# A two-layer recurrent trunk on one core: the o and v projections of head groups 2 and 3 as seven block products in place of eight, with the residual kept in DRAM

## The chip, the cores and the metric

The kernel runs on one core of one Trainium2 chip. The metric is the device time of one execution in microseconds. The kernel before takes 1529.73 us, the median of 3 runs (1529.43 to 1530.63).

## What is computed

Input `x` has 256 tokens of 2048 channels. Two layers follow, each a matrix-memory branch (A) and a gated linear recurrence (B) side by side, and then a last RMS norm. Everything is float32. Cut to what matters:

```python
def hybrid_layer(x, ...):
    u = rms_norm(x, norm_g)
    p = u @ w_in                              # 2048 x 12304
    qk, v, o, z_a, ig, fg, xb, z_b = split(p) # 2048 each; ig, fg 8 each
    q, k = split(silu(causal_dwconv(qk, qk_conv)))
    h = mlstm_chunkwise(q, k, v, ig + i_bias, log_sigmoid(fg + f_bias))
    h = h * sigmoid(o)
    y_a = norm_per_head(h) * head_norm_g * silu(z_a)
    xc = causal_dwconv(xb, lru_conv_w) + lru_conv_b
    y_b = rg_lru(xc, w_a, b_a, w_x, b_x, lam) * silu(z_b)
    return x + concat(y_a, y_b) @ w_out       # 4096 x 2048

def reference(x, ...):
    for l in range(2): x = hybrid_layer(x, ...)
    return rms_norm(x, final_g)
```

The o and v of the diff are the columns of `w_in` that give the output gate `o` and the values `v`. There are 8 heads of 256 columns, worked on as 4 groups g of 2 heads, so o and v of one group are two products of the same 256 x 2048 left factor with 2048 x 512.

## The kernel before, in words

**Weights.** All weights lie in DRAM as units of 1 MB (`ws[u]`, 128 partitions x 2048), in the order in which the kernel uses them. The queue of SyncE (SP) loads one unit after another into `raw`, three buffers of 1 MB (L204). A unit is two halves of 128x1024. `prepare` (L209) splits each half into two numbers of lower precision: ScalarE (ACT) casts it to `wH` (L222) and VectorE (DVE) subtracts that from `raw`, which leaves `wL` (L223, recorded as L111, the line of the helper `tt_`). `wH` and `wL` have four buffers each, so a half's buffer is the one of the half four places earlier, and a cast or a subtraction waits until TensorE (PE) is through with that one. The main loop prepares three halves ahead.

**Products.** A product of float32 numbers is three products of split numbers: high x high, high x low and low x high. `mm_a` (L238 to L240; o, v, z and the output projection) keeps a 128x128 block of the activations in the array and streams 512 columns of weights: 12 matmuls of 512 columns for a half. `mm_b` (L255 and L257; qk, xb and zb) keeps the weights and streams the activations: 8 pairs of a 512 and a 256 column matmul for a half. o, v, z, qk, xb and zb are chunks of 4 units each; one chunk of the output projection is 2 units.

**Accumulators.** The 8 PSUM banks are two pairs `acc` (128 x 2 x 512) for the chunks and four single banks for everything else. A chunk takes the pair that the chunk before it does not have.

**Order.** `_plan` (L31) lists the chunks. For each layer and group: o, v, qk, one chunk of the output projection of the group before, xb, a second, z, gate, a third, zb, a fourth. What follows a chunk is its post (`o_post` L432, `v_post` L442, `qk_post` L457, `z_post` L525, `gate_half` L583, `zb_post` L648); the longer ones are generators, which the main loop advances a little after each half (`pump`). The residual stays in SBUF: `out_chunk` (L685) adds its accumulator into `x_acc` (128 x 2 x 2048) on DVE. `y_a` and `y_b`, the left factors of the output projection, have two buffers each (`yaH`, `yaL`, `ybH`, `ybL`). `gate_half` makes the two gates of the recurrence: for each of 8 blocks of 128x256 matmuls of 512 and 256 columns, a bias on ACT (L601), an addition on DVE, and one sigmoid over 1024 columns (L604).

From this a scheduler makes the order of instructions of each engine. An engine takes its own in that order, one after another.

Of the kernel before, what the change touches and what calls it, by code (L numbers as in the profile page):

```python
# [27 lines left out]
AHEAD = 3  # L28


def _plan():  # L31
    plan = []
    for l in range(DEPTH):
        for g in range(NG):
            fill = [("out", l, g - 1, c) for c in range(4)] if g > 0 else []
            late = [("in", l, "zb", 0)]
            plan += [("in", l, "o", g)] + (late if g == 1 else []) + [("in", l, "v", g), ("in", l, "qk", g)]
            plan += fill[0:1] + [("in", l, "xb", g)] + fill[1:2] + [("in", l, "z", g), ("gate", l, g)]
            if g > 0:
                plan += fill[2:3] + [("in", l, "zb", g)] + fill[3:4]  # L40
        if l + 1 < DEPTH:
            plan += [("out", l, NG - 1, c) for c in range(4)]
        else:
            plan.append(("last", l, NG - 1))
    return plan
# [3 lines left out]
def tile_trunk(ctx, tc, x, xt, par, gw, gb, ws, final_g, out):  # L49
# [10 lines left out]
    ps_main = ctx.enter_context(tc.tile_pool(name="ps_main", bufs=2, space=PSUM))  # L60
    ps_aux = ctx.enter_context(tc.tile_pool(name="ps_aux", bufs=4, space=PSUM))

    def aux(name):
        return ps_aux.tile([P, 512], F32, tag="aux", name=name)
# [5 lines left out]
    x_acc = act.tile([P, 2, D], F32, tag="xacc", name="x_acc")  # L70
# [15 lines left out]
    def load_x(c):  # L86
# [6 lines left out]
        nc.sync.dma_start(out=x_acc[:, :, cs], in_=xv[:, :, cs])  # L93
        square_sum(c)
        if c == 3:
            st["x_in"] = True
# [9 lines left out]

    gwp = const.tile([P, KT, 104], F32R, name="gwp")
    G.memset(gwp.bitcast(F32), 0.0)
# [12 lines left out]
    def log1p_exp_half(x_, tl):  # L121
        """returns q with log1p(exp(-|x|)) = 2 q"""
# [64 lines left out]
    st = {"nload": 0, "credit": 0.0}  # L187

    def load_unit(n):
        raw = wraw.tile([P, 2048], F32, tag="raw", name="raw")  # L190
        u = st["nload"]
        st["nload"] += 1
        if n < 4:
# [9 lines left out]
    def add_unit(mms, before=None, after=None):  # L203
        box = {}  # L204
        for i in range(2):
            halves.append(dict(box=box, i=i, mm=mms[i], split=None,
                               before=before if i == 0 else None, after=after if i == 1 else None))

    def prepare(hf):  # L209
        n = len(xT_parts) if hf["i"] == 0 else 1  # L210
        if hf["i"] == 0:
            hf["box"]["raw"] = load_unit(n)
            if n < 4:
                split_xT(0, n, xT_parts[n], range(4 * n, 4 * n + 4))
            if 4 <= st["nload"] < 8:
                load_x(st["nload"] - 4)
# [4 lines left out]
        for o in range(0, 1024, w):  # L221
# [39 lines left out]
    def chunk_in(l, kind, g, postfn, beforefn=None):  # L261
        def make_acc():
            box = {}

            def acc():
                if "t" not in box:
                    box["t"] = ps_main.tile([P, 2, 512], F32, tag="acc", name="acc")
# [43 lines left out]
    def square_sum(c):  # L311
        for t in range(2):
            junk = work.tile([P, 512], F32, tag="sF", name="junk")
            S.activation(out=junk, in_=x_acc[:, t, 512 * c : 512 * c + 512], func=AF.Square,
# [27 lines left out]
    def gates(l):  # L342
        gr = gwr[l]
        for s in range(2):
            hs, ls = slice(32 * s, 32 * s + 8), slice(64 + 32 * s, 72 + 32 * s)
            S.copy(out=gwp[:, :, hs], in_=gr[:, :, 8 * s : 8 * s + 8])
            tt_(gwp[:, :, ls], gr[:, :, 8 * s : 8 * s + 8], gwp.bitcast(F32)[:, :, hs], ALU.subtract)

    def gates_mm(l):
        ps = aux("ps_g")  # L350
        o = ps[0:104, 0:T]
        for kt in range(KT):
            PE.matmul(o, gwp[:, kt, :], st["x"][:, kt, 0, :], start=kt == 0, stop=False)
            PE.matmul(o, gwp[:, kt, :], st["x"][:, kt, 1, :], start=False, stop=kt == KT - 1)
        st["ps_g"] = ps

    def gates_gen(l):
        ps, rb = st["ps_g"], st["rb", l]

        def sc(nm):  # L360
            return small.tile([NH, T], F32, tag=f"sc_{nm}", name=f"sc_{nm}", bufs=1)
# [17 lines left out]
        sT = small.tile([64, T], F32, tag="sT", name="sT", bufs=1)  # L379
# [586 lines left out]
```

## Time and profile before

| | us |
|---|---|
| median of 3 runs | 1529.73 |
| span of the profiled execution | 1528.4 |
| PE busy | 1510.9 |
| DVE busy | 1127.6 |
| ACT busy | 885.4 |
| POOL busy | 37.6 |

The profiled execution's own time isn't given apart; its span is 1.3 us under the median of the runs, and what lies around the span is put at that. Busy shares are averages over the whole span. In a list of groups each row has the line, the engine, the operation, the tiles out<-in and the count, then busy time and the mean ns of one, then the idle time of the engine ahead of these instructions with what ended it. A row of the list of waits has the idle total, the number of waits and the longest. A row of the table of windows has the stretch, its length, the busy time of each engine with the number of instructions, the granted clock of TensorE, the share of DMA time in use and GB/s.

### The profile page before, as it was taken

Reading aid. Unit: us, or ns where it says so; the run is one execution under the profiler, and the core shown is the slowest. Engines: PE = TensorE matmul, PEld = TensorE weight load, DVE = VectorE, ACT = ScalarE, POOL = GpSimd, SP = SyncE. Lnnn points to the kernel's source line nnn. Section 1 sums busy time; section 2 is a strip of 40 time slices with the busy share of each in tenths; the row PEclk is TensorE's granted clock in tenths of the full one; section 3 lists DMA queues with packets and bytes.
Section 4 is the critical chain, followed back from the end, with each engine's and each line's share of the span. In section 5 each row is a group of like instructions: output and inputs, shape, how many; then the busy total and the mean of one; then the engine's idle time right before and its main releaser. Section 6 shows DMA issues by size and latency. Waiting matters only on the chain.

```text
span 1528.4 us, 19659 instructions
## 1 busy us (share of the span) xinstructions
PE 1510.9 (99%) x7576; PEld 1278.2 (84%) x7576; DVE 1127.6 (74%) x1594; ACT 885.4 (58%) x1141; POOL 37.6 (2%) x109
## 2 busy tenths in 40 slices
PE   8999999999999999999999999999999999999997
PEld 6888888888888888888888888888888888888885
DVE  6888867794677847778658787777847887478874
ACT  7567654674547645575555485557544575444854
POOL 0000100000000000000000001000000000000002
PEclk9999999999999999999999999999999999999998
DMA  9554655455554555445555555545555455555562
GB/s 344 192 188 164 212 185 182 173 196 194 188 190 171 191 193 193 175 183 193 175 184 180 190 176 193 193 173 192 193 193 185 173 184 197 187 182 187 171 223 102
DMA packets 45117, 288.03 MB, mean 188 GB/s; under 512 B 5072, under 2 KB 7648, under 8 KB 11744
## 3 DMA queue, kind: packets, MB, share of 16 engines
q1 hardware_dynamic: 43600, 283.40, 52.4%
q0 software_dynamic: 992, 3.16, 0.7%
q8 instruction: 59, 0.97, 0.3%
q14 instruction: 34, 0.28, 0.1%
q10 hardware_dynamic: 432, 0.23, 0.0%
HBM read 284.66 MB, written 2.11 MB: 188 GB/s over the span
## 4 chain that ended last, share of the span: by engine, by line
PE 98%; ACT 1%; DMA 0%; DVE 0%; SPq 0%; issue 0%; ACTq 0%
PE acc L255 24%; PE acc L238 18%; PE acc L240 18%; PE acc L239 18%; PE acc L257 12%; PE ps_gt L595 2%; PE ps_gt L597 1%; PE acc L788 0%; PE acc L790 0%; PE acc L789 0%; PE ps_ty L551 0%; DMA raw<-in_ws_dram 0%; PE acc_x L790 0%; PE acc_x L788 0%; PE acc_x L789 0%; PE ps_n L428 0%
## 5 line engine op out<-in xcount | busy, mean ns | idle before, releaser
L222 ACT CAST wH<-raw 128x1024 fp32r<-128x1024 f32 (+1 forms) x529 | 554.0, 1049 | 567.6 <-PE acc L240 282.6
L111 DVE TENSOR_TENSOR wL<-raw,wH 128x1024 fp32r<-128x1024 f32 (+1 forms) x529 | 643.8, 1220 | 312.3 <-ACT wH L222 311.5
L255 PE MATMUL acc<-x_s,wH 128*128 128x512 f32 x1536 | 544.1, 399 | 0.0
L257 PE MATMUL acc<-x_s,wL 128*128 128x256 f32 x1536 | 431.2, 281 | 0.0
L255 PEld LDWEIGHTS acc<-x_s,wH 128*128 128x128 f32 x1536 | 288.6, 188 | 71.0
L238 PE MATMUL acc<-wH,x_s 128*128 128x512 f32 x768 | 301.0, 392 | 6.7 <-ACT wH L222 6.7
L239 PE MATMUL acc<-wL,x_s 128*128 128x512 f32 x768 | 300.2, 391 | 0.3 <-DVE wL L111 0.3
L240 PE MATMUL acc<-wH,x_s 128*128 128x512 f32 x768 | 299.8, 390 | 0.0
L257 PEld LDWEIGHTS acc<-x_s,wL 128*128 128x128 f32 x1536 | 290.1, 189 | 0.9
L238 PEld LDWEIGHTS acc<-wH,x_s 128*128 128x128 f32 x768 | 144.7, 188 | 36.2 <-ACT wH L222 6.7
L239 PEld LDWEIGHTS acc<-wL,x_s 128*128 128x128 f32 x768 | 144.7, 188 | 30.3 <-DVE wL L111 1.2
L240 PEld LDWEIGHTS acc<-wH,x_s 128*128 128x128 f32 x768 | 144.6, 188 | 30.1
L238 PE MATMUL acc<-wH,ybH 128*128 128x512 f32 x224 | 88.1, 393 | 0.0
L238 PE MATMUL acc<-wH,yaH 128*128 128x512 f32 x224 | 87.8, 392 | 0.0
L239 PE MATMUL acc<-wL,yaH 128*128 128x512 f32 x224 | 87.4, 390 | 0.0
L240 PE MATMUL acc<-wH,yaL 128*128 128x512 f32 x224 | 87.4, 390 | 0.0
L240 PE MATMUL acc<-wH,ybL 128*128 128x512 f32 x224 | 87.3, 390 | 0.0
L239 PE MATMUL acc<-wL,ybH 128*128 128x512 f32 x224 | 87.2, 389 | 0.0
L238 PEld LDWEIGHTS acc<-wH,yaH 128*128 128x128 f32 x224 | 42.0, 188 | 9.1
L240 PEld LDWEIGHTS acc<-wH,yaL 128*128 128x128 f32 x224 | 42.1, 188 | 8.9
L240 PEld LDWEIGHTS acc<-wH,ybL 128*128 128x128 f32 x224 | 42.0, 188 | 8.8
L238 PEld LDWEIGHTS acc<-wH,ybH 128*128 128x128 f32 x224 | 42.1, 188 | 8.4
(201 smaller groups left out, 1437.2 us busy)
## 6 DMA issues: line engine op xcount, KB each, us to landing
raw<-in_ws_dram SPq DMA_DIRECT2D x260, 1024.0 KB, 4.8
raw<-in_ws_dram SPq DMA_DIRECT2D x6, 512.0 KB, 7.9
xp<-in_xt_dram SPq DMA_DIRECT2D x8, 256.0 KB, 7.4
x_acc<-in_x_dram SPq DMA_DIRECT2D x4, 512.0 KB, 9.7
nb<-nG_d POOLq DMA_DIRECT2D x8, 256.0 KB, 3.7
out_dram<-x_acc SPq DMA_DIRECT2D x8, 256.0 KB, 3.0
raw<-in_ws_dram SPq DMA_DIRECT2D x4, 256.0 KB, 6.3
fg<-in_final_g_dram POOLq DMA_DIRECT2D x2, 512.0 KB, 4.5
```

Of the source, the lines that this page charges most:

```text
L111: return V.tensor_tensor(out=o, in0=a, in1=b, op=op)
L222: S.copy(out=H[:, o : o + w], in_=r[:, o : o + w])
L238: PE.matmul(ps[:, t, :], a_H[:, kt, tsl], Hv[:, k, :], start=s, stop=False)
L239: PE.matmul(ps[:, t, :], a_H[:, kt, tsl], Lv[:, k, :], start=False, stop=False)
L240: PE.matmul(ps[:, t, :], a_L[:, kt, tsl], Hv[:, k, :], start=False, stop=e)
L255: PE.matmul(ps[:, ct, :], Hv[:, k, csl], xs[:, kt].rearrange("p a t -> p (a t)"), start=s, stop=False, skip_group_check=True)
L257: PE.matmul(ps[:, ct, T : 2 * T], Lv[:, k, csl], xs[:, kt, 0, :], start=False, stop=e, skip_group_check=True)
L595: PE.matmul(ps, Hv[:, ib, jl], xs[:, ib].rearrange("p a t -> p (a t)"), start=i == 0, stop=False, skip_group_check=True)
L597: PE.matmul(ps[:, T : 2 * T], Lv[:, ib, jl], xs[:, ib, 0, :], start=False, stop=i == 1, skip_group_check=True)
```

## The change

**Order.** `_plan` is replaced by `_sequence`, which orders units instead of chunks. A group has a head (o, zb of group 0 in group 1, and v; without o and v in groups 2 and 3) and a body: qk, two chunks of the output projection of the group before, xb, the other two, z, gate, zb. In the bodies of groups 1 and 2 stand, spread between, 16 side units: `swB` and then `swA` of the next group. After every two units of the body come one or two of them.

**Seven products for eight.** `swB` and `swA` compute o and v of group 2 or 3 together. For a pair of rows of blocks of 128 (`kp`, 8 of them) the left factor is a 2x2 array of blocks (two blocks of tokens, two of channels) and the right one too (two blocks of channels; the columns of o and those of v). Three of the seven products are in `swB` and four in `swA`, each in three terms (`sw_mm`), so a unit has 9 and 12 matmuls of 512 columns, and the eight pairs of one layer and group 168 instead of 192. The left factors' sums are made once per layer by `sw_forms` (16 operations of 1024 columns and 32 of 256 in both layers on DVE, and 8 casts on ACT), into the tile of `x_acc`. The right factors' sums are partly made in DRAM ahead of time: `stage_copy` issues 64 copies of 256 KB from DRAM to DRAM on ACT's queue and `stage_add` 64 accumulating transfers of 256 KB on POOL's; the `swA` units make two more with two additions of 128x512 on DVE. `sw_post` adds up the results: for each group 1 copy on ACT and 9 operations of 128x512 on DVE.

**PSUM.** During a pass (`swB` or `swA`) one pair `acc` and two of the four other banks belong to it, and all chunks of the body take the remaining pair. When the pass is over, the next chunk takes the pair that the pass had (`new_acc`).

**Residual in DRAM.** `out_chunk` of groups 0 to 2 copies its accumulator to `stage` (one buffer) on ACT and adds it to `xd[c]` in DRAM with an accumulating transfer of 512 KB on POOL's queue, 24 in all. Ahead of the gate of group 3 `x_acc` is loaded again on SP's queue.

**Smaller parts.** `yaH`, `yaL`, `ybH` and `ybL` have one buffer each; the tile of the gate weights is put into two of these. `gate_half` uses three matmuls of 256 columns instead of one of 512 and one of 256, and takes the sigmoid straight from PSUM, so the bias step, the addition and the wide sigmoid go. `pump`'s budget is halved in halves of a side unit.

```diff
-    ps_main = ctx.enter_context(tc.tile_pool(name="ps_main", bufs=2, space=PSUM))
-    ps_aux = ctx.enter_context(tc.tile_pool(name="ps_aux", bufs=4, space=PSUM))
+    psum = ctx.enter_context(tc.tile_pool(name="psum", bufs=1, space=PSUM))
+    def aux(name):
+        st["aux"] = 1 if st["sw"] else 1 - st["aux"]
+        return psum.tile([P, 512], F32, tag=f"aux{st['aux']}", name=name, bufs=2)
+    def new_acc():
+        st["pair"] = 1 - st["sw"]["pair"] if st["sw"] else 1 - st["pair"]
+        return psum.tile([P, 2, 512], F32, tag=f"acc{st['pair']}", name="acc")
+    def sw_banks():
+        pair = 1 - st["pair"]
+        a = psum.tile([P, 2, 512], F32, tag=f"acc{pair}", name="sacc")
+        b = [psum.tile([P, 512], F32, tag="aux0", name=f"sacc{i}", bufs=2) for i in range(2)]
+        st["sw"] = {"pair": pair, "banks": [a[:, 0, :], a[:, 1, :]] + b}
...
+    def load_x_acc():
+        new_x_acc()
+        for c in range(4):
+            nc.sync.dma_start(out=st["xa"][:, :, 512 * c : 512 * c + 512], in_=xd[c])
...
+    def load_unit(n, item, j):
...
+        if item[0] == "swA":
+            uo = blocks[("in", item[1], "o", item[2]), j // 2]
+            nc.sync.dma_start(out=raw[:, 0:1024], in_=ws[uo][:, 1024 * (j % 2) : 1024 * (j % 2) + 1024])
+            nc.sync.dma_start(out=raw[:, 1024:1536], in_=pq[item[1:]][j][:, 512:1024])
+            tt_(raw[:, 0:512], raw[:, 0:512], raw[:, 1024:1536], ALU.add)
+            tt_(raw[:, 1536:2048], raw[:, 0:512], raw[:, 512:1024], ALU.add)
+            return raw
...
     def gate_half(l, g, which):
...
-                        PE.matmul(ps, Hv[:, ib, jl], xs[:, ib].rearrange("p a t -> p (a t)"), start=i == 0,
-                                  stop=False, skip_group_check=True)
-                        PE.matmul(ps[:, T : 2 * T], Lv[:, ib, jl], xs[:, ib, 0, :], start=False, stop=i == 1,
-                                  skip_group_check=True)
+                        for W, a in ((Hv, 0), (Hv, 1), (Lv, 0)):
+                            PE.matmul(o, W[:, ib, jl], xs[:, ib, a, :], start=j == 0 and i == 0 and W is Hv and a == 0,
+                                      stop=i == 1 and W is Lv, skip_group_check=True)
...
     def out_chunk(l, g, c):
...
+            if g < NG - 1:
+                stage = act.tile([P, 2, 512], F32, tag="stage", name="stage")
+                S.copy(out=stage, in_=ps)
+                G.dma_start(out=xd[c], in_=stage, accum_op=ALU.add)
+                return
...
+    def sw_mm(bank, aH, aL, H, L, first, last):
+        PE.matmul(bank, aH, H, start=first, stop=False)
+        PE.matmul(bank, aH, L, start=False, stop=False)
+        PE.matmul(bank, aL, H, start=False, stop=last)
...
+    def sw_post(l, g, which):
+        m = st["sw"]["banks"]
+        st["sw"] = None
+        if which == "B":
+            e = st["swe"] = act.tile([P, 3, 512], F32, tag="swe", name="swe")
+            S.copy(out=e[:, 0, :], in_=m[0])
+            tt_(e[:, 1, :], m[1], e[:, 0, :], ALU.subtract)
+            tt_(e[:, 2, :], m[2], e[:, 1, :], ALU.add)
+            st["credit"] -= 1.3
+            return
+        require(("lru", l, g - 1))
+        require(("ybT", l, g - 1))
+        e = st["swe"]
+        t = work.tile([P, 512], F32, tag="sC", name="swt")
+        tt_(t, e[:, 0, :], m[1], ALU.add)
+        tt_(e[:, 0, :], e[:, 0, :], m[0], ALU.add)
+        tt_(e[:, 1, :], e[:, 1, :], m[1], ALU.subtract)
+        tt_(e[:, 2, :], e[:, 2, :], m[1], ALU.subtract)
+        tt_(t, t, m[2], ALU.add)
+        tt_(e[:, 1, :], e[:, 1, :], m[2], ALU.subtract)
+        tt_(t, t, m[3], ALU.add)
...
+    def stage_copy(d, b):
+        for h in range(2):
+            S.dma_start(out=d[:, 512 * h : 512 * h + 512], in_=b[0][1])
+    def stage_add(d, b):
+        for h in range(2):
+            G.dma_start(out=d[:, 512 * h : 512 * h + 512], in_=b[h][h], accum_op=ALU.add)
...
+        if hf["i"] == 0:
+            k = (n // 2 - STAGE_FROM) // STAGE_EVERY
+            if n // 2 >= STAGE_FROM and (n // 2 - STAGE_FROM) % STAGE_EVERY == 0:
+                if k < len(staged):
+                    stage_copy(*staged[k])
+                if 0 < k <= len(staged):
+                    stage_add(*staged[k - 1])
```

**How the order of instructions moves: the end of a pass.** DVE in the changed kernel where the `swA` pass of group 2, layer 0, ends and qk of group 2 begins. `zb`, `zsg` and `ybL` are the post of zb of group 1 in two parts, `sacc_2916` is the pass's pair, `swt` and `swe` the sums of `sw_post`; `wL_3634` and `wL_3648` are the second half of the first unit of qk and the first of the second.

```order
L178 TENSOR_TENSOR wL_3634<-raw_3606,wH_3633 128x1024
L178 TENSOR_TENSOR zb_3499<-zb_3499,acc_3536 128x512
L178 TENSOR_TENSOR ybL_3501<-zb_3499,ybH_3500 128x512
L178 TENSOR_TENSOR zb_3499<-zb_3499,rb_466 128x512
L178 TENSOR_TENSOR wL_3648<-raw_3645,wH_3647 128x1024
L178 TENSOR_TENSOR zsg_3663<-zb_3499,zsg_3663 128x512
L178 TENSOR_TENSOR swt_3669<-swe_2908,sacc_2916 128x512
L178 TENSOR_TENSOR zb_3499<-zsg_3663,xc_2712 128x512
L178 TENSOR_TENSOR swe_2908<-swe_2908,sacc_2916 128x512 x2
L178 TENSOR_TENSOR ybL_3501<-zb_3499,ybH_3500 128x512
L178 TENSOR_TENSOR swe_2908<-swe_2908,sacc_2916 128x512
```

The same engine before, where v of group 2 ends and its qk begins (`wL_3315` is the first half of qk):

```order
L111 TENSOR_TENSOR wL_3297<-raw_3278,wH_3296 128x1024
L111 TENSOR_TENSOR wL_3315<-raw_3312,wH_3314 128x1024
L111 TENSOR_TENSOR wL_3331<-raw_3312,wH_3330 128x1024
L111 TENSOR_TENSOR wL_3349<-raw_3346,wH_3348 128x1024
L114 SCALAR_TENSOR_TENSOR vL_3365<-acc_3231,rstd_378,vH_3364 128x2x256
L111 TENSOR_TENSOR wL_3375<-raw_3346,wH_3374 128x1024
L114 SCALAR_TENSOR_TENSOR vL_3365<-acc_3231,rstd_378,vH_3364 128x2x256
```

Before, two operations of the post stood among the subtractions; now ten stand between `wL_3634` and the last read of the pass's pair, with one subtraction between them.

**PE at the same place**, the last matmuls of the pass (`wH_3558` and `wH_3581` are its last two halves) and the first of qk, with the semaphores that an instruction waits on:

```order
L857 MATMUL sacc_2916<-wH_3558,x_s_106 128x512
L855 MATMUL sacc0_2917<-wH_3581,sf_788 128x512 [waits Activation_49]
L856 MATMUL sacc0_2917<-wL_3582,sf_788 128x512 [waits DVE_49]
L857 MATMUL sacc0_2917<-wH_3581,sf_788 128x512
L855 MATMUL sacc1_2918<-wH_3581,x_s_106 128x512
L856 MATMUL sacc1_2918<-wL_3582,x_s_106 128x512
L857 MATMUL sacc1_2918<-wH_3581,x_s_106 128x512
L342 MATMUL acc_3696<-x_s_106,wH_3608 128x512 [waits DVE_49,Activation_49]
L344 MATMUL acc_3696<-x_s_106,wL_3609 128x256
```

and before, the last of v and the first of qk:

```order
L238 MATMUL acc_3231<-wH_3296,x_s_107 128x512
L239 MATMUL acc_3231<-wL_3297,x_s_107 128x512
L240 MATMUL acc_3231<-wH_3296,x_s_107 128x512
L255 MATMUL acc_3378<-x_s_107,wH_3314 128x512 [waits Activation_49]
L257 MATMUL acc_3378<-x_s_107,wL_3315 128x256 [waits DVE_49]
```

The first matmul of qk now waits for DVE as well as for ACT: its pair is the one that `sw_post` reads last in the piece of DVE's order above. Before, its pair was the one that o had had, four units back.

**ACT early in layer 0**, around the qk chunk of group 0 (`pq...` are the DRAM buffers of the staged sums; `padt` is the first read of qk's accumulator). Now:

```order
L309 CAST wH_672<-raw_670 128x1024 [waits DMAHW1_49,PE_49,Activation_49]
L1041 DMA pq030_115<-in_ws_dram 128x512 [waits DMAHW2_49]
L1041 DMA pq030_115<-in_ws_dram 128x512 [waits DMAHW3_49]
L416 COPY padt_692<-acc_602 128x2x256 [waits PE_49]
L309 CAST wH_718<-raw_670 128x1024 [waits DVE_49]
L1041 DMA pq031_116<-in_ws_dram 128x512 [waits DMAHW4_49]
L1041 DMA pq031_116<-in_ws_dram 128x512 [waits DMAHW5_49]
```

and before:

```order
L222 CAST wH_639<-raw_637 128x1024 [waits DMAHW3_49,PE_49,Activation_49]
L222 CAST wH_685<-raw_637 128x1024 [waits DVE_49,PE_49]
L329 COPY padt_659<-acc_565 128x2x256 [waits PE_49]
L222 CAST wH_708<-raw_706 128x1024 [waits DMAHW4_49,DVE_49,PE_49]
```

In the source the copies begin at unit 12 and come every second unit; in the order that results they stand between the casts of layer 0's first units, two for a half, and wait on semaphores of earlier transfers.

More of the change, by code (lines that the diff above doesn't have):

```diff
@@ L39, in _plan @@
[L39 to L40 removed]
+            body = [("in", l, "qk", g)] + fill[0:2] + [("in", l, "xb", g)] + fill[2:4]
+            body += [("in", l, "z", g), ("gate", l, g)] + ([("in", l, "zb", g)] if g > 0 else [])
+            side = [("swB", l, g + 1), ("swA", l, g + 1)] if (l, g + 1) in SW else []
+            seq += spread(head, []) + spread(body, side)
         if l + 1 < DEPTH:
[L42 to L44 removed]
@@ L689, in acc @@
             if "t" not in box:
[L690 removed]
+                box["t"] = new_acc()
             return box["t"]
```

243 lines of the change are left out of this document (180 added, 63 removed).

## The prediction

> **What bounds the kernel now.** I read the page first, its busy times and its chain, then the groups that occupy DVE and ACT, then the list of waits, which tells whether those engines are late or are held up.
>
> ```profile
> span 1528.4 us, 19659 instructions
> PE 1510.9 (99%) x7576; PEld 1278.2 (84%) x7576; DVE 1127.6 (74%) x1594; ACT 885.4 (58%) x1141; POOL 37.6 (2%) x109
> PE 98%; ACT 1%; DMA 0%; DVE 0%; SPq 0%; issue 0%; ACTq 0%
> L238 PE MATMUL acc<-wH,x_s 128*128 128x512 f32 x768 | 301.0, 392 | 6.7 <-ACT wH L222 6.7
> ```
> ```profile
> DVE wL L111 <- ACT wH L222: 311.5, 300, 2.8
> ACT wH L222 <- PE acc L240: 282.6, 186, 2.7
> ACT wH L222 <- PE acc L255: 208.4, 149, 2.1
> POOL padt L336 <- DVE qc L114: 426.8, 14, 67.0
> ```
>
> The chain is PE for 98%, and its commonest product waited 6.7 us in all, at the start. ACT's casts wait for PE (282.6 + 208.4 us) and DVE's subtractions for those casts. So PE is the bound and the other two are ahead of it by as much as four buffers let them be: removed matmuls come off the time in full, as long as the buffers stay full. What drains them is a place where DVE or ACT has more to do than PE, within the three or four halves that they are ahead.
>
> A busy row of PE overlaps its neighbours (392 ns), so I take the pace from two stretches without a wait: an `mm_a` stretch, then an `mm_b` stretch, first with all instructions on the accumulators, then with L255 alone.
>
> ```profile
> 306.16:311.38 5.22, 5.22 (x24) 4.32 (x23) 0.00 (x0) 0.00 (x0) 1.00 0.85 281
> 311.38:322.67 11.29, 11.29 (x65) 9.79 (x64) 1.21 (x1) 0.00 (x0) 1.00 0.50 179
> 311.38:322.67 11.29, 11.29 (x32) 5.94 (x32) 1.00 0.50 179
> ```
>
> 5.22 us over 23 steps is 0.227 us for a matmul of 512 columns; 11.29 over 32 pairs is 0.353 for 512 + 256, which leaves 0.126 for 256. A half is 12 x 0.227 = 2.72 or 8 x 0.353 = 2.82 us.
>
> **The change part by part.** The durations, DVE's groups and then ACT's:
>
> ```profile
> L111 DVE TENSOR_TENSOR wL<-raw,wH 128x1024 fp32r<-128x1024 f32 x527 | 642.4, 1222 | 310.3 <-ACT wH L222 309.4
> L111 DVE TENSOR_TENSOR zb<-zb,acc 128x512 f32<-128x512 f32 x16 | 10.9, 683 | 0.5
> L111 DVE TENSOR_TENSOR gate<-gate,ps_gt 128x256 f32<-128x256 f32 x64 | 24.7, 413 | 8.4 <-ACT gate L601 8.4
> L222 ACT CAST wH<-raw 128x1024 fp32r<-128x1024 f32 x527 | 552.8, 1051 | 565.5 <-PE acc L240 282.6 <-PE acc L255 208.4 <-issue 36.4
> L601 ACT ACTIVATE gate<-ps_gt,pars 128x256 f32<-128x256 f32 x64 | 26.9, 477 | 2.6 <-PE ps_gt L597 2.6
> L604 ACT ACTIVATE gate<-gate 128x1024 f32<-128x1024 f32 x16 | 17.0, 1061 | 0.0
> ```
>
> *Matmuls removed.* 192 - 168 = 24 of 512 columns for each of four layer-groups: 96 x 0.227 = **-22 us**. The gate's 128 pairs become 384 matmuls of 256: 384 x 0.126 - 128 x 0.353 = 48.4 - 45.2 = **+3** (0 to 3).
>
> *Work added on DVE.* 64 halves with 32 x 1.22 + 32 x 0.69 more of subtraction (61), 64 additions of raw weights and 36 of the results at 0.683 (68), the left sums at 16 x 1.22 + 32 x 0.41 (33); taken away are the gate's additions (25) and 24 additions of the residual at 1.22 (29). Sum +107, so DVE goes from 1128 to about 1235 us of 1530. On average that lies beside PE. ACT gets 32 casts of 1024 and 32 of 512, 24 copies, and loses 27 + 17 - 64 x 0.48 in the gate; it ends near 1000 with its new issues and does not bind on average either. So what counts are the places.
>
> *The ends of the passes.* The first piece of DVE's order, above, is the costliest. The buffer of `wL_3634` is that of zb's last half. When PE is through with that, all it has left is the pass's last two halves, 2 x 6 matmuls or 2.72 us, since `acc_3696`, the first of qk, needs the pair that `sw_post` reads in the last row of that piece. By then there have to run the cast for `wL_3634` (1.05), two subtractions (2 x 1.22) and ten operations of 128x512 (10 x 0.683): 10.3 us. PE waits 10.3 - 2.7 = 7.6 us. In the list of groups instructions that follow at once overlap by some 50 ns (96 of `qc` in 40.6 us at a mean of 479 ns), which would take 0.6 off; two casts of `ybH` in the way would add 0.6 each:
>
> ```profile
> L114 DVE SCALAR_TENSOR_TENSOR qc<-padt,pars,qc 128x256 f32<-128x256 f32 x96 | 40.6, 479 | 0.1
> L668 ACT CAST ybH<-zb 128x512 fp32r<-128x512 f32 x16 | 9.9, 617 | 1.8 <-DVE zb L111 1.8
> ```
>
> The least is the six reads of the pair alone, 4.1, less the 1.36 us of the last half, 2.7; the most 8.8. Nearest to what stands in the order is 8. All four `swA` passes end like this: **+32** (11 to 35). At the end of v, before, two operations stood in the same place and the pair wasn't the one just read.
>
> *One pair for the body.* During a pass a chunk begins when the post of the chunk before has read the same pair. The last half's copy off PSUM has a cast and a subtraction in front of it: 1.05 + 1.22 + 0.68 = 2.95 us, and the cover is a `swB` unit of 9 x 0.227 = 2.04 or a `swA` unit of 2.72. That leaves 0.9 about three times in each of four bodies: **+11** (0, where the post comes first, to 20, where ACT's copy to `stage`, 1.05, comes on top at the chunks of the output projection). Where `swB` gives its banks to `swA`, a copy and two additions, 0.58 + 2 x 0.68, stand against the two units between: **+3** (0 to 6).
>
> *The left sums.* 33 us of DVE in two stretches of layer start. For layer 0:
>
> ```profile
> 0.00:40.00 40.00, 33.00 (x134) 26.50 (x135) 26.10 (x51) 29.04 (x53) 2.66 (x13) 1.00 0.94 347
> 40.00:60.00 20.00, 20.00 (x108) 17.27 (x107) 13.77 (x24) 13.30 (x17) 0.11 (x1) 1.00 0.48 173
> 60.00:80.00 20.00, 20.00 (x115) 17.16 (x114) 18.24 (x32) 10.00 (x13) 1.72 (x4) 1.00 0.49 167
> 80.00:100.00 20.00, 20.00 (x116) 17.32 (x115) 16.97 (x28) 13.34 (x18) 2.30 (x6) 1.00 0.67 228
> 100.00:145.00 45.00, 44.94 (x229) 37.88 (x228) 37.33 (x77) 29.31 (x40) 0.76 (x3) 1.00 0.49 170
> ```
>
> DVE (third of the busy times) has 18.24 + 16.97 + 37.33 = 72.5 of the 85 us from 60 to 145, so 12.5 are free for 16.6: 4 over, if the generators are let out over the whole stretch. For both layers **+3** (0 to 8).
>
> *Staging.* The table's last two columns are the share of DMA time and GB/s. Loads alone take all there is in the first 40 us (347 GB/s at 0.94, so 369 at 1.0), and about half later. Ahead of 145 us they move 347 x 40 + 173 x 20 + 167 x 20 + 228 x 20 + 170 x 45, or 32.9 MB. The change puts 56 of its 64 copies between the casts of that stretch, 14.7 MB, as many additions can follow, and four stores of the residual move 2.1: 64.4 MB, 174 us of transfer in 145, 29 over. PE needs only the loads, and SP runs up to three units ahead; but if three queues shared evenly, loads would get 123 of the 170 GB/s that they need for 14.7 MB / 0.123 = 120 us, 5.6 MB short or 33 us. The 56 issues cost ACT itself 24 us, at 0.43 from the row below, in a stretch where it is busy two thirds. The end of the range is 0, when the additions move past 145 us, and 40. Copies come two by two behind a cast, so they can't flood the queue: I take a third, **+11**.
>
> ```profile
> 0.81 0.43 ACTq L75 DMA_DIRECT2D pars<-in_par_dram  x1
> raw<-in_ws_dram SPq DMA_DIRECT2D x260, 1024.0 KB, 4.8
> x_acc<-in_x_dram SPq DMA_DIRECT2D x4, 512.0 KB, 9.7
> L409 POOL DMA_DIRECT2D nb<-nG_d x8 | 4.4, 554 | 89.5 <-DVE E L119 84.3 <-DMA nG_d<-sc_d 5.2
> ```
>
> The Trainium skill (Collectives: The Full Stack, "The bandwidth ceiling: the fold count and why AG ≠ RS ≠ AR") speaks against this part: an addition made by the DMA has to read two sources, so it puts twice the read traffic of a copy on the queue. By that the additions would weigh another 14.7 MB, 79.1 in all or 214 us of transfer in 145, 69 over instead of 29, and by the same third the sum would be 13 higher. No row of before has such a transfer.
>
> *At nothing.* One buffer for each y: the output projection of the group before has ended when z of this one begins, since its chunks now stand ahead of z; were it not so, `yaH` would wait a chunk, 11 us, each time. The two halves of the gate weights lie in `yaH` and `yaL` at the start of a layer, ahead of the first z. The reload of `x_acc` is four issues on SP and four landings of 9.7 us, a few units before the output projection that reads it. Third issues for a side unit lie on SP, which does nothing else.
>
> The sum: -22 + 3 + 32 + 11 + 3 + 3 + 11 = +41. The profiled span is 1.3 us below the median, so against the median **1570 us**. With the terms' ends not all on one side I hold 1545 to 1600 for this case.
>
> **The rivals.**
>
> *Faster, PE alone decides.* DVE's generators come early enough that `sw_post` starts with nothing ahead of it, and the one pair is read in time. For it: between 60 and 80 us DVE is busy 18.24 of 20 and PE has no gap. Against it: that stretch has the posts spread, while here twelve operations are lined up between two dependent halves. The pass ends and the one pair would have to cost nothing: -22 + 3 and 5 for staging and sums, 1516.
>
> *The staging saturates DMA.* As the even share above, 33 instead of 11, and ACT held in front of a copy that waits for an earlier transfer (the `DMAHW` waits in the last pieces of the order), so that casts stand behind it: 56 issues with 0.2 each, another 11. 1570 + 22 + 11, about 1603. For it are the rows at 0.94; against it that PE lost nothing there between 40 and 60 us.
>
> *The residual's one stage.* `out_chunk` copies into a buffer that must have landed in DRAM: 1.05 + 0.55 to issue + 9.7 (the row of 512 KB) is 11.3 us, while two chunks of the projection follow at 4 x 2.72 or less plus the side units, some 9 to 12. POOL's issues also stand behind its memsets, which wait up to 67.0 us for DVE in the list of waits. A second chunk held for 2 us, 12 times, with ACT's casts behind the copy: +25, 1595.
>
> *It balances.* Pass ends at 4 x 4, half of what they are above, and the left sums at 3, with no wait elsewhere, give -22 + 3 + 16 + 3 = 0: 1530.
>
> **How the numbers follow.** The forecast 0.55, staging 0.20, the one stage 0.07, faster 0.13, balance 0.05. The range of 8 in 10 reaches from 1524, which leaves out most of the faster case, to 1612. A difference of 0.2%, 3 us, is about what a measurement of this kernel can tell from none. Of the balance case 0.03 fall within it and 0.02 above: faster 0.13, same 0.03, slower 0.84.
>
> **What would show it.** PE busy falls by some 19 us while its idle time rises by about 60. Right: qk's first matmul after each `swA` pass waits about 8 us for DVE, in four places; waits of 1 us at first matmuls of body chunks; nothing but small waits for `raw` after 145 us. Wrong: PE waiting for casts which wait for `raw` (staging), a long wait of ACT's copy to `stage` for a transfer, or pass ends of 2 us and a PE that stays at 99%.

## The result, and the profile after

The changed kernel takes 1652.82 us, the median of 4 runs (1647.36 to 1654.66), against 1529.75 before: 1.0798 times as long, 95% interval 1.0785 to 1.0811, or 123 us more.

The page of the changed kernel, its busy times, the granted clock and DMA's share in 40 slices, two of the DMA queues (packets, MB, share of the DMA engines' time) and the chain of waits:

```profile
span 1652.9 us, 20593 instructions
PE 1527.1 (92%) x7608; PEld 1277.0 (77%) x7608; DVE 1217.2 (74%) x1722; ACT 949.3 (57%) x1226; POOL 113.5 (7%) x200
PEclk9996899999999999999999999999999999999998
DMA  9899998667546676477565544576764766547752
q0 software_dynamic: 13664, 32.53, 11.5%
q10 hardware_dynamic: 11824, 21.21, 4.2%
PE 67%; DMA 15%; DVE 11%; ACT 4%; issue 2%; SPq 0%; ACTq 0%; DVEq 0%; POOL 0%; POOLq 0%
```

The chain was PE for 98%. Now DMA has 15% of it and DVE 11%. DMA is full in the first seven slices, some 280 us, where before it was so in the first alone. The window of those 280 us, of the changed kernel and then of the one before (length, busy time of PE, PEld, DVE, ACT and POOL with counts, granted clock, DMA share, GB/s):

```profile
0.00:280.00 280.00, 213.63 (x995) 175.05 (x996) 168.12 (x273) 133.71 (x186) 63.75 (x97) 0.91 0.99 285
```
```profile
0.00:280.00 280.00, 272.94 (x1385) 231.02 (x1386) 215.56 (x346) 173.73 (x236) 12.50 (x38) 1.00 0.59 208
```

In the same time PE did 995 matmuls instead of 1385, while DVE and ACT have less to do too. No engine there has too much to do; they wait. PE is idle for 66.4 us instead of 7.1, and its granted clock is 0.91 instead of 1.00, which is worth at most 0.09 x 280 = 25 us: 59 and 25 make 84. One event can be measured alike in both: the first matmul on `yaH`, the output projection's first chunk, starts at 307.4 us, and at 224.2 before. So 83 us of the 123 are lost by then. Waits of the changed kernel, of the whole span:

```profile
POOL pq L1045 <- DMA pq<-in_ws_dram: 161.9, 54, 12.0
ACT stage L799 <- PE acc L327: 35.8, 21, 2.8
PE acc L342 <- DVE swe L178: 29.8, 4, 7.5
PE acc L344 <- DVE wL L178: 26.5, 6, 22.0
```

`swe` is the pass ends, four waits. The wait of 22.0 us is one event in the first 280 us. DVE's and PE's timelines there, and POOL's (start, duration, line, operation, in brackets the idle time ahead and its releaser):

```profile
113.98 0.42 DVE L178 TENSOR_TENSOR sff<-xf,sff 128x256 f32<-128x256 f32 x1
138.37 0.35 DVE L186 TENSOR_SCALAR E<-nb,aT 128x256 f32<-128x256 f32 x1 [23.97 <-DMA nb<-nG_d]
...
141.05 0.58 PE L344 MATMUL acc<-x_s,wL 128*128 128x256 f32 x1 [21.95 <-DVE wL L178]
```
```profile
115.83 0.82 POOL L483 DMA_DIRECT2D nG_d<-scs  x1
117.39 0.81 POOL L1045 DMA_DIRECT2D pq<-in_ws_dram  x1 [0.74 <-DMA pq<-in_ws_dram]
121.91 0.81 POOL L1045 DMA_DIRECT2D pq<-in_ws_dram  x1 [3.71 <-DMA pq<-in_ws_dram]
130.66 0.61 POOL L505 DMA_DIRECT2D nb<-nG_d  x1 [7.94 <-DMA nG_d<-scs]
```

A row of gate values of 8 KB goes out to DRAM and comes back (`nG_d`, then `nb`, which DVE needs). In POOL's order the additions stand in between. The 8 KB take from 115.83 to 130 us, and `nb` until 138.37; DVE, which takes its instructions in order, stands still for 24 us with a subtraction for PE behind that one operation. The profile fits the rival on staging, and goes past its price.

### The profile page after: what moved, and what is told of

It reads as the page before. It is cut to its first block, busy times and chain, and to the rows that moved or that the text cites. A ratio compares the mean times of both kernels' runs of the same rounds, so it can differ in the third digit from the quotient of the medians.

```text
span 1652.9 us, 20593 instructions
## 1 busy us (share of the span) xinstructions
PE 1527.1 (92%) x7608; PEld 1277.0 (77%) x7608; DVE 1217.2 (74%) x1722; ACT 949.3 (57%) x1226; POOL 113.5 (7%) x200
## 4 chain that ended last, share of the span: by engine, by line
PE 67%; DMA 15%; DVE 11%; ACT 4%; issue 2%; SPq 0%; ACTq 0%; DVEq 0%; POOL 0%; POOLq 0%
PE acc L342 19%; PE acc L326 10%; PE acc L325 10%; PE acc L327 10%; PE acc L344 9%; DVE wL L178 5%; DMA pq<-in_ws_dram 5%; DMA raw<-pq 5%; ACT wH L309 2%; PE ps_gt L693 2%; DMA raw<-in_ws_dram 1%; DMA x_acc<-in_x_dram 1%; PE sacc L856 1%; PE sacc L857 1%; PE sacc L855 1%
## 5 line engine op out<-in xcount | busy, mean ns | idle before, releaser
L178 DVE TENSOR_TENSOR wL<-raw,wH 128x1024 fp32r<-128x1024 f32 (+1 forms) x593 | 700.8, 1191 | 281.7 <-ACT wH L309 279.2
L309 ACT CAST wH<-raw 128x1024 fp32r<-128x1024 f32 (+1 forms) x593 | 602.7, 1027 | 510.8 <-PE acc L342 177.9
L342 PE MATMUL acc<-x_s,wH 128*128 128x512 f32 x1536 | 554.1, 403 | 37.9 <-DVE swe L178 29.8
L344 PEld LDWEIGHTS acc<-x_s,wL 128*128 128x128 f32 x1536 | 295.0, 192 | 30.0 <-DVE wL L178 29.6
L325 PE MATMUL acc<-wH,x_s 128*128 128x512 f32 x512 | 204.3, 399 | 19.0 <-ACT wH L309 15.3
L326 PE MATMUL acc<-wL,x_s 128*128 128x512 f32 x512 | 204.7, 400 | 6.2 <-DVE wL L178 6.2
L327 PE MATMUL acc<-wH,x_s 128*128 128x512 f32 x512 | 203.5, 397 | 0.0
L325 PEld LDWEIGHTS acc<-wH,x_s 128*128 128x128 f32 x512 | 98.6, 193 | 41.7 <-ACT wH L309 17.5
L326 PEld LDWEIGHTS acc<-wL,x_s 128*128 128x128 f32 x512 | 98.2, 192 | 30.9 <-DVE wL L178 11.1
L327 PEld LDWEIGHTS acc<-wH,x_s 128*128 128x128 f32 x512 | 98.5, 192 | 20.0
L178 DVE TENSOR_TENSOR raw<-raw 128x512 f32<-128x512 f32 x64 | 44.2, 691 | 53.2 <-DMA raw<-pq 52.7
L1045 POOL DMA_DIRECT2D pq<-in_ws_dram x64 | 52.6, 854 | 166.4 <-DMA pq<-in_ws_dram 161.9
L856 PE MATMUL sacc<-wL,sf 128*128 128x512 f32 x128 | 50.7, 396 | 1.1 <-DVE wL L178 1.1
```

The source lines that it names most:

```text
L178: return V.tensor_tensor(out=o, in0=a, in1=b, op=op)
L309: S.copy(out=H[:, o : o + w], in_=r[:, o : o + w])
L325: PE.matmul(ps[:, t, :], a_H[:, kt, tsl], Hv[:, k, :], start=s, stop=False)
L326: PE.matmul(ps[:, t, :], a_H[:, kt, tsl], Lv[:, k, :], start=False, stop=False)
L327: PE.matmul(ps[:, t, :], a_L[:, kt, tsl], Hv[:, k, :], start=False, stop=e)
L342: PE.matmul(ps[:, ct, :], Hv[:, k, csl], xs[:, kt].rearrange("p a t -> p (a t)"), start=s, stop=False, skip_group_check=True)
```

## The experiments

Each is one edit of the changed kernel (or of the run named). There are twelve runs. The sums on DVE and the sums on POOL were timed four times, the others once; the kernel before took 1529.7 to 1529.8 beside them. The four times of the changed kernel lie 7.3 us apart, and those with the sums on DVE 9.1, so a few us between two single times say little.

**No staging.** The copies and additions in DRAM are out, and blocks of the same size are loaded in their place.

```diff
-            nc.sync.dma_start(out=raw[:, 1024:1536], in_=pq[item[1:]][j][:, 0:512])
+            nc.sync.dma_start(out=raw[:, 1024:1536], in_=even[1])
...
-            nc.sync.dma_start(out=raw[:, 1024:1536], in_=pq[item[1:]][j][:, 512:1024])
+            even, odd = sw_blocks(item, j)
+            nc.sync.dma_start(out=raw[:, 1024:1536], in_=even[1])
...
-                if k < len(staged):
-                    stage_copy(*staged[k])
-                if 0 < k <= len(staged):
-                    stage_add(*staged[k - 1])
+                pass
```

> The 64 copies and the 64 accumulating transfers that stage sums in DRAM are left out; the side units load an unsummed block of the same size in their place, so the output is not the reference's. Theory: the first 280 us lose 83 us to these transfers (the first chunk of the output projection of group 0 starts at 307.4 us instead of 224.2 before), so the time falls by about 83 to 1570 and that chunk starts at 224 to 235. Rival: the start is slow because of the left sums on DVE, the stores of the residual and the one PSUM pair; then it stays above 1630 and the chunk starts later than 285.

1585.8 us, 67 less: 16 above the theory's 1570, and far below the rival's 1630. The first chunk starts at 231.9 us, as the theory had it, and the window is again nearly what it was before:

```profile
0.00:280.00 280.00, 271.28 (x1377) 228.34 (x1378) 221.35 (x359) 176.41 (x239) 16.15 (x42) 1.00 0.64 224
```

All but 7.7 us of the loss up to that chunk (231.9 against 224.2) is the staging's. The time fell by 8 less than that chunk's start did: behind it, PE's waits for `wL` sum to 14 us instead of 10 with staging, and the half clock after the four pass ends lasts 34 us instead of 27.

**Which part of the staging.** Three edits, each alone: the additions left out; the additions made plain writes; the copies issued by POOL.

```diff
-                if 0 < k <= len(staged):
-                    stage_add(*staged[k - 1])
```
```diff
-            G.dma_start(out=d[:, 512 * h : 512 * h + 512], in_=b[h][h], accum_op=ALU.add)
+            G.dma_start(out=d[:, 512 * h : 512 * h + 512], in_=b[h][h])
```
```diff
-            S.dma_start(out=d[:, 512 * h : 512 * h + 512], in_=b[0][1])
+            G.dma_start(out=d[:, 512 * h : 512 * h + 512], in_=b[0][1])
```

> The 64 copies on ACT's queue stay, the 64 accumulating transfers are left out, so the staged blocks are copies without a sum. In the changed kernel, between 60 and 270 us, the accumulating queue took 41% of the DMA time for 14.9 MB, the copies 24% for 15.1 MB, the loads 34%. Theory (the DMA engines are full and the additions are the dear ones): without them 86 us of transfer time go and the loads fit again: 1586 to 1605. Rival (ACT and SP are held by waits on semaphores shared with the copies): half of the 67 us that leaving out all staging won stays, 1620 or more.

> The 64 transfers on POOL's queue write instead of adding; count, bytes, order and waits as in the changed kernel, but the staged blocks hold no sum. Theory (the price is the DMA time of an accumulating transfer, 86 us for 14.9 MB, where a copy takes 51 us for 15.1 MB): they cost like the copies, the three queues ask for some 175 of 210 us, and most of the 67 us go: 1590 to 1615. Rival (what costs is the number of transfers and the waits in ACT's and POOL's order): 1635 or more.

> All 128 staging transfers as in the changed kernel, but the copies are issued by POOL too, so ACT issues none of them. Output as the reference's. Theory (DMA time): the same bytes are moved early, 1630 to 1660. Rival (casts standing behind copies in ACT's order, 12 us at most for one, and SP's loads behind semaphores shared with the copies): 1595 to 1620.

1595.7, 1630.7 and 1676.6 us. So the copies alone cost 10 us, as their theory had it, a second set of 64 writes beside them 35 more, and making those additions another 22. The plain writes lie between theory (1615) and rival (1635). The last run is 24 us slower than the changed kernel, beyond the theory's 1660 too, and PE's longest wait in it is 32.4 us instead of 22.0, with all 128 transfers in the order in which POOL issues `nb`. So nothing is won by taking the copies off ACT. That they cost nothing on ACT isn't shown by it: in the changed kernel ACT stood for 30 us, in five places, behind a wait for a staging transfer, and PE waited behind one of these (ACT's wait, then PE's row):

```profile
ACT qks L566 <- DMA pq<-in_ws_dram: 8.8, 1, 8.8
198.62 0.58 PE L524 MATMUL ps_S<-qks 128*128 128x256 f32 x1 [7.46 <-ACT qks L566]
```

DMA between 60 and 270 us, of the changed kernel (packets, MB, share of the 210 us; then KB each and median us to landing), and the two staging queues of the run with plain writes:

```profile
q0 software_dynamic: 7987, 14.86, 41.1%
q1 hardware_dynamic: 3831, 27.92, 34.0%
q10 hardware_dynamic: 8301, 15.14, 24.3%
...
raw<-in_ws_dram SPq DMA_DIRECT2D x26, 1024.0 KB, 9.2
pq<-in_ws_dram ACTq DMA_DIRECT2D x55, 256.0 KB, 15.9
```
```profile
q10 hardware_dynamic: 8120, 14.78, 24.3%
q0 software_dynamic: 4672, 15.22, 22.9%
```

q0 carries POOL's transfers. Adding took 0.411 x 210 / 14.86 = 5.8 us of DMA time for a MB, writing 3.2 on the same queue, the copies 3.4, a load (q1) 2.6. A unit's load landed after 9.2 us instead of 4.8.

The Trainium skill (Collectives: The Full Stack, "The bandwidth ceiling: the fold count and why AG ≠ RS ≠ AR") says of reductions between ranks that an addition needs two source reads. 5.8 to 3.2 is 1.8 times the DMA time for the same bytes, here within one core, which agrees.

**Staging spread out.** Each copy is held back by a write of 4 KB from a weight half of its time, and stands every fourth unit.

```diff
-STAGE_FROM, STAGE_EVERY = 12, 2
+STAGE_FROM, STAGE_EVERY = 10, 4
...
-                    stage_copy(*staged[k])
+                    S.dma_start(out=staged[k][0][0:1, :], in_=hf["split"][0].bitcast(F32)[0:1, :])
                 if 0 < k <= len(staged):
-                    stage_add(*staged[k - 1])
+                    stage_copy(*staged[k - 1])
+                if 1 < k <= len(staged) + 1:
+                    stage_add(*staged[k - 2])
```

> The same 64 copies and 64 accumulating transfers, each copy held back by a small write of 4 KB that needs a weight half of its time, one sum every four units from unit 10 on, so over some 140 units instead of the first 50. Theory (DMA saturated at the start): at an added load of some 0.2 of DMA's time beside the 0.5 of the weights it costs under 15 us: 1570 to 1585. Rival (every copy and addition costs by holding ACT, POOL or a shared semaphore, wherever it stands): the 83 us stay, 1640 or more.

1609.4 us. 43 of the 67 us go: crowding at the start is the larger part. 24 stay, between theory and rival: transfers cost where they are spread out too, at a DMA share of six to nine tenths in the first 19 of the 40 slices.

**The pass ends.** After `swA` the next chunk takes the pair that the body had.

```diff
         st["credit"] -= 4.8
+        st["pair"] = 1 - st["pair"]
```

> After a swA pass the next chunk takes the pair that the body had, not the one that sw_post reads; all else as in the changed kernel. Theory: the four waits of 7.43 to 7.47 us go, and with them about 2 us each of the half clock that follows such a wait (10 matmuls at 0.64 us a pair in place of 0.35): 1653 - 38 = 1615. Rival: DVE is 7 us behind all the same and PE meets it a few matmuls later at the next wL, so that only 0 to 12 us are won: 1641 or more.

1618.4 us, 34.4 less, and the four waits are gone. They had looked like this in the changed kernel; first DVE's timeline, then PE's first matmul of qk, then the windows around it (the last three columns as above):

```profile
468.25 1.22 DVE L178 TENSOR_TENSOR wL<-raw,wH 128x1024 fp32r<-128x1024 f32 x1
469.38 0.68 DVE L178 TENSOR_TENSOR zb<-zb,acc 128x512 f32<-128x512 f32 x1
...
474.12 1.28 DVE L178 TENSOR_TENSOR swe<-swe,sacc 128x512 f32<-128x512 f32 x2
475.32 0.69 DVE L178 TENSOR_TENSOR ybL<-zb,ybH 128x512 fp32r<-128x512 f32 x1
475.92 0.69 DVE L178 TENSOR_TENSOR swe<-swe,sacc 128x512 f32<-128x512 f32 x1
```
```profile
476.75 0.77 PE L342 MATMUL acc<-x_s,wH 128*128 128x512 f32 x1 [7.43 <-DVE swe L178]
```
```profile
470.00:475.00 5.00, 0.00 (x0) 0.00 (x0) 5.00 (x9) 2.27 (x4) 0.11 (x1) 0.89 0.64 211
475.00:480.00 5.00, 3.25 (x10) 2.80 (x11) 5.00 (x9) 2.63 (x4) 0.00 (x0) 0.50 0.00 0
480.00:485.00 5.00, 5.00 (x29) 4.38 (x28) 2.10 (x3) 1.67 (x2) 0.00 (x0) 0.93 0.58 208
```

The piece of DVE's order that stands ahead of the prediction runs off without a gap from 468.25 on, and PE's matmul begins as its last row ends. The granted clock then is 0.5 for 6.8 us (2 x (0.11 + 0.50 + 0.07) x 5), of which PE works about four, and so loses two.

**The pieces together.** The same edit without staging, and the same again without the sums of blocks and results on DVE (64 additions and 36 operations, 68 us of DVE; o and v then read raw banks).

```diff
-            tt_(raw[:, 0:512], raw[:, 0:512], raw[:, 1024:1536], ALU.add)
-            tt_(raw[:, 1536:2048], raw[:, 0:512], raw[:, 512:1024], ALU.add)
...
-        tt_(t, e[:, 0, :], m[1], ALU.add)
...
-        o_post(l, g, (e[:, 0, :], t))
-        v_post(l, g, (e[:, 2, :], e[:, 1, :]))
+        o_post(l, g, (m[0], m[1]))
+        v_post(l, g, (m[2], m[3]))
```

> Staging left out as in the first run (output not the reference's) and the other pair after a swA pass, all sums on DVE as in the changed kernel. It tells how far the terms add up. Theory (staging and pass ends are two places that have nothing to do with one another): 1585.8 - 34.4 = 1551, within 3. Rival (with the pair free, DVE's lateness moves to the next places, as it did with the sums on DVE): 1560 or more.

> No staging, the other pair after a pass, and DVE without the sums of the right factors (64 additions) and of the results (36 operations): 68 us of DVE less than in the changed kernel; ACT's 4 copies of results go too. The products, their banks and their order on PE stay, o and v read raw banks, so the output is not the reference's. From 1585.8 without staging the other pair should take 34. Theory (what is left in the bodies is DVE being late: 14 us of waits for wL in the run without staging): 1525 to 1542. Rival (what is left is the one pair of the bodies and the order of PE): 1548 or more.

1556.2 and 1524.7 us. The first missed the sum by 5 and lies between theory and rival. The second is the only one below before (1529.8), by 5 us in one run, and without those sums it is no replacement. PE's waits in the first, then in the second:

```profile
PE acc L345 <- DVE wL L178: 9.2, 8, 1.6
PE acc L327 <- DVE wL L178: 6.2, 11, 1.2
PE acc L343 <- DVE padt L178: 4.2, 4, 1.3
PE sacc L857 <- DVE wL L178: 2.4, 4, 0.9
```
```profile
PE acc L341 <- DVE padt L178: 3.3, 4, 0.9
PE acc L324 <- DVE padt L178: 3.1, 7, 0.8
PE acc L325 <- DVE wL L178: 0.3, 1, 0.3
```

Some 18 us of waits for `wL` in 23 places become 0.3 us in one place when DVE has 68 us less. What is left in the bodies is the one pair (`padt`, and 1.8 us for `zb`).

This edit takes more from DVE than work. The sums of the right factors read a unit that has just been loaded, and DVE takes its instructions in order, so it stands still until the load has landed, with subtractions for PE behind the addition. In the first of the two runs (DVE's waits of the whole span, then DVE's and PE's timelines):

```profile
DVE raw L178 <- DMA raw<-in_ws_dram: 55.7, 24, 4.8
313.24 0.69 DVE L178 TENSOR_TENSOR raw<-raw 128x512 f32<-128x512 f32 x1 [4.34 <-DMA raw<-in_ws_dram]
315.13 0.50 PE L327 MATMUL acc<-wL,ybH 128*128 128x512 f32 x1 [0.69 <-DVE wL L178]
```

Between 300 and 340 us, where this is, DVE is busy for only 24 of 40 us. 14 of PE's late places, 10 of the 18 us, come right behind an addition that had waited for its load. In the second run that standing is gone together with the 68 us of work, so the two are not told apart.

**Three attempts to keep the products and pay less**, all with the output of the reference. The sums of right factors on DVE, loading the four raw blocks, with the other pair; the same sums on POOL; and the first of these with the second half of each qk, xb and zb accumulator copied by ACT.

```diff
-            nc.sync.dma_start(out=raw[:, 1024:1536], in_=pq[item[1:]][j][:, 0:512])
+            nc.sync.dma_start(out=raw[:, 1024:1536], in_=even[1])
+            tt_(raw[:, 1024:1536], raw[:, 1024:1536], raw[:, 0:512], ALU.add)
...
-            nc.sync.dma_start(out=raw[:, 1024:1536], in_=pq[item[1:]][j][:, 512:1024])
+            uv = blocks[("in", item[1], "v", item[2]), j // 2]
+            nc.sync.dma_start(out=raw[:, 1024:2048], in_=ws[uv][:, 1024 * (j % 2) : 1024 * (j % 2) + 1024])
+            tt_(raw[:, 1024:1536], raw[:, 1024:1536], raw[:, 1536:2048], ALU.add)
```
```diff
+        ev = work.tile([P, 2, T], F32, tag="ev", name="ev")
         S.copy(out=o, in_=acc[:, :, 0:T])
-        tt_(o, o, acc[:, :, T : 2 * T], ALU.add)
+        S.copy(out=ev, in_=acc[:, :, T : 2 * T])
+        tt_(o, o, ev, ALU.add)
```

> No staging: the side units load the four raw blocks (1 MB as a plain unit) and DVE adds them, one more addition of 128x512 in each side unit (64 in all, 44 us of DVE), and the next chunk takes the other pair as in the run before. The output is the reference's. Theory: 1653 - 83 - 38 = 1532, plus 0 to 15 where the bodies' DVE is late: 1532 to 1547, so no gain over before (1529.7). Rival: the added 44 us of DVE come out in full at the bodies, 1570 or more; or the sum of both fixes hides more than it should, under 1525.

> As the run with sums on DVE and the other pair (1584.6), but the 128 additions of raw blocks of 128x512 are done by POOL, and POOL's small fills of padt, vH and vL go to DVE. Output as the reference's. Theory (DVE is what is late in the bodies): 88 us of DVE go from four bodies and the time falls to 1535 to 1555. Rival (POOL's additions, 1.34 us each by the trace of before and three in a row, and their order behind its own waits make raw late): 1590 or more.

> The run with sums on DVE and the other pair (1584.6), but the second half of each qk, xb and zb accumulator is copied off PSUM by ACT (48 more copies of 128x512) and DVE adds it from SBUF, so a pair comes free without waiting for DVE. Output as the reference's. Theory (chunks of a body wait for the one pair because its last reader stands in DVE's order): the waits for padt and zb at first matmuls, 20 us in that run, fall to a few: 1565 to 1575. Rival (ACT's copies delay its casts by as much): 1582 or more.

> The three mends together, output as the reference's: staging spread over 140 units, the other pair, and the second half of each accumulator copied by ACT. If they add up, 1609.4 - 34.4 - 17.8 = 1557, still slower than before (1529.8), since the sums of the right factors and of the results stay on DVE. Rival (the spread transfers cost through ACT's order, where 48 more copies now stand): 1567 or more.

The sums on DVE: 1584.6 (1577.5 to 1586.6), 1.0349 times before, 1.0320 to 1.0378. Theory missed by some 40 us, and the rival's 1570 or more held, though the added work did not come out in full: against the run without staging and with the other pair, 44 us more of DVE cost 28. On POOL: 1585.1, 1.0367 times, 1.0349 to 1.0384, no better, and between theory and rival. POOL's additions there, and DVE's subtractions at the same time:

```profile
L263 POOL TENSOR_TENSOR raw<-raw 128x512 f32<-128x512 f32 x128 | 212.5, 1660 | 551.4 <-DMA raw<-in_ws_dram 468.2 <-DVE zb L178 29.1 <-DVE wL L178 10.2
L178 DVE TENSOR_TENSOR wL<-raw,wH 128x1024 fp32r<-128x1024 f32 x559 | 719.0, 1298 | 245.5 <-ACT wH L315 239.3 <-PE sacc L863 3.5
```

A subtraction took 1298 ns on average instead of 1220 with the sums on DVE, 44 us over 559 of them; two at 381.5 us, beside three of POOL's additions, took 4.54 us. DVE's other operations grew longer too, and POOL's fills came to it, so all of the 88 us was given back: DVE is busy for 1255.0 us, and with the sums on DVE 1254.7. The theory, which had DVE with 88 us less, was not put to the test. With ACT's copies: 1566.8 us, 17.8 less than the sums on DVE, as its theory had it: PE's 23 us of waits for `padt` and `zb` become 3 for ACT's copies. It is the fastest of those whose output is the reference's, and still 37 above before. The last expectation is of the three mends together (spread staging, the other pair, ACT's copies): 1590.2 against 1557 expected. With ACT's copies and the spread transfers in one kernel PE waited 22.5 us for `wL` at the low products instead of 5.5 in the spread run alone. The rival held; that ACT's order is the reason was not shown.

## Why the prediction was wrong, step by step

The chain of runs that differ by one edit gives the whole: staging 1652.8 - 1585.8 = 67.0, pass ends 1585.8 - 1556.2 = 29.6, the sums on DVE 1556.2 - 1524.7 = 31.5, and all the rest 1524.7 - 1529.8 = -5.1. The sum is 123.0. Three of the runs in it are single ones.

**Direction** was right: slower, by places and not by averages. The time was not; it lies outside the range. Nor was the order of the terms: the pass ends stood as the costliest, and came third. PE busy was to fall by some 19 us; it rose by 16.2, as matmuls at half clock last longer.

**Staging, +11: the step that failed most, 67.** Two things in it were wrong. "29 over" counted bytes at the speed of a load, 369 GB/s or 2.7 us of DMA time for a MB; the copies took 3.4 and the additions 5.8. And "I take a third" rested on copies that "can't flood the queue" and on a PE that "needs only the loads". The DMA share was 0.99 for 280 us and a copy landed after 15.9 us; and the loads are not all: `nb`, 256 KB for DVE, stood behind additions in POOL's order and on full DMA engines, 24 us in one wait. The rival had 33 by shared queues and 11 for ACT, 44 in all; its mechanism, full DMA, was right and its price too low. Of its part on ACT one wait of PE, 7.5 us, shows in the trace. The Trainium skill's two source reads would have given 24 in place of 11, by the working in the prediction, which is in the right direction and no better a size.

How much of the 67 is full engines and how much instructions that wait in order behind late transfers stays open: the copies and plain writes need some 110 us of DMA time, by their 3.4 and 3.2 us for a MB, and 280 x (1 - 0.59) = 115 were free, yet they cost 45 us.

**Work added on DVE, "on average that lies beside PE": the second step that failed, 0 against 31.5.** The instructions were counted nearly rightly (+107 us of DVE forecast, 1217.2 - 1127.6 = 89.6 measured). But only lateness at pass ends, left sums and the one pair had a price; in the bodies, where 68 us more stand in four stretches, the subtractions come late in 22 places by 0.8 us on average. The additions' waits for their loads, 55.7 us in which DVE does nothing, are not in the prediction at all; how much of the 31.5 is work and how much these waits stays open. The waits named sum to 18; PE idle in all differs by 22.4 between the two runs, PE busy by 9.1; short waits that lie inside a matmul's record could explain that, which isn't shown.

**Pass ends, +32:** mechanism and size right. 7.6 us each were worked out, 7.43 to 7.47 came, 29.8 together. The half clock behind each was not in the sum; the edit won 34.4 with staging and 29.6 without. That 29.6 is so near to 29.8 is luck: PE's idle time fell by 22.6 only, as some 7 us of lateness came back at later places, and its busy time by 7.0, with a granted clock of 0.998 instead of 0.987.

**Removed matmuls, -22 + 3.** The gate's change is nothing: in the chain 23 of its matmuls take

```profile
430.63 2.71 PE ps_gt L693 x23
```

0.118 each, 384 of them 45.2 us, as much as before. With hardly any wait left PE busy was 1496.7, 14 below before instead of 22, and the time 5 below; where the other 8 are stays open.

**One pair and the handover, +14:** waits for `padt` are 6.5 us in the run without staging, so half the size and within the ends given.

**Left sums, +3:** with the residual's stores 7.7 us up to the first chunk of layer 0, at the upper end of what was given for both layers.

**The residual's one stage** did not happen: ACT's copy waits for PE (35.8 us), never for the transfer, which landed in 5.3 us at the median, not 9.7. The faster rival's 1516 was not reached even without staging, with the other pair and with 68 us less on DVE (1524.7).

## What to carry to other kernels

When the bound engine is at 99%, products saved there are worth their time only if the engines that feed it have the added work to spare in the same stretch; price the added work at the rate of the stretch where it stands, not of the span. Ask too what an added operation waits for: one that reads a load holds up what stands behind it in its engine's order, though the engine has time to spare. Price background transfers in DMA time of their own kind, which for an accumulating one was twice that of a load, and look for small transfers on the critical path that share their queue. After a pass that borrows an accumulator, give the next chunk the one that was read longest ago: that one line was worth 30 us.

## What the runs showed of the hardware

The granted clock can halve after waits that are short. In the run with sums on DVE a wait of 1.82 us, some 15 us after one of 2.42, was followed by (windows, then PE's row):

```profile
294.00:298.00 4.00, 4.00 (x12) 3.11 (x11) 3.68 (x6) 1.09 (x2) 0.00 (x0) 0.58 0.86 274
...
293.67 0.51 PE L328 MATMUL acc<-wH,yaH 128*128 128x512 f32 x1 [1.82 <-DVE padt L178]
```

4 us at a mean of 0.58, that is 3.4 at half, which costs 1.7: as much as the wait itself. The length of the wait alone doesn't decide it. In the same run the clock stayed at 1.00 after the 2.42 us, and from 610 to 618 us, behind a longer wait:

```profile
610.29 0.38 PE L347 MATMUL acc<-x_s,wL 128*128 128x256 f32 x1 [3.36 <-DVE wL L178]
```

The Trainium skill (TensorE: Matmul & The Clock Gate, "Part 1: The HAM clock gate (the "warmup" mystery)") has a free-running window of about 3.4 us in which activity is judged. The 3.4 us here and 6.8 at the pass end are one and two of these, which agrees. The Trainium skill's rule on the same page, under "HAM oscillation — how this bites in real kernels", to keep gaps under about 3.4 us, is too loose here: 1.82 was enough.
